# A hybrid decoder block: where the attention groups are combined, and how early four kinds of loads are asked for

## The chip, the cores and the metric

The kernel runs on one core of a Trainium2 chip. The metric is the time of one execution on the device in microseconds; the kernel before takes 2662.7 us (median of three runs, 2660.01 to 2666.11). A core has a matrix engine (TensorE, PE in the profile, its weight loads PEld), a vector engine (DVE), an activation engine (ACT), a general engine (POOL) and a queue engine (SP). Each works through its own queue in order; they wait for each other through semaphores. DMA transfers are issued from the queues of SP, ACT and POOL.

## What is computed

The reference is one layer on 2048 tokens of width 1024, in float32. From `h = rmsnorm(x)` one projection gives q, k, v for 12 heads, u and z for a gated unit, and two gates:

```
q, k = rope(...), rope(...);  u = gelu(...);  z = gelu(...)
gate_a, gate_b = sigmoid(...), sigmoid(...)
for g, (window, dilation) in enumerate(((128,1), (512,4), (2048,16))):
    o[g], lse[g] = dilated_window_attention(q[g], k[g], v[g])
y_attn = sum_g softmax_g(lse)[g] * o[g]                     # "combine"
y_gmlp = u * (tril(w_spatial) @ layernorm(z) + b_spatial)   # per chunk of 128 tokens
merged = gate_a * (y_attn @ w_branch_attn) + gate_b * (y_gmlp @ w_branch_gmlp)
x = x + rmsnorm(merged @ w_out)
x = x + rmsnorm(relu(rmsnorm(x) @ w_mlp_in)**2 @ w_mlp_out)
```

## The kernel before

Every large product is made in three matmuls of 128x512 from operands split in a high and a low part (`split`, line 68: the high part by one engine at L70 or L72, the low part at L78; `mm3`, L95 to L97). The tokens are worked on in four chunks of 512, numbered 0 to 3, two halves of two chunks. PE's order is written out by hand: each helper yields after three matmuls, and a call `steps(n)` takes n such steps from a generator (`filler`) that holds the projections for u, z and the gates. The order of the other engines is made by a planner from the order in the program, its own clock and what each instruction waits for; `behind()` makes what it holds come after the last instruction traced so far on each of these engines.

The stages in the order of time:

1. q, k and v of all tokens (up to about 470 us), then u and z of the second half.
2. `gates()` (L703): u and gate projections that are left, 126 pieces `t` of 12 matmuls, some with sums of operands that save products (phases `PHASES`). A piece's weights are loaded by `piece` (L627, four pieces ahead) and split by `split_piece` (three ahead) into places of two tiles `spots`, `t % 8`, or `t % 4` in the last phase, which starts at `LAST` = 116. A finished bank is copied by ACT (L722, `i == 1`) or added by DVE (L727 to L741) and stored (L717). One more load from the list `ins` goes out per piece (L720). From step 12 of it on, the attention's 48 units run between these steps, each a chain PE, DVE, ACT, PE.
3. When attention is done (about 958 us), 75 steps of the gates are left. `combined` there interleaves them with `combine(c)` of chunks 2 and 3: five parts, which load `A` (L961), form the factors (L964 to L977), scale (ACT L982, DVE L985), add (L987, L988), and transpose on PE (L993) and store `ya` (ACT L996, L997).
4. z of the first half: two chunks of 32 steps of PE, with its weights `w_z0` and the operand `hT_b` reloaded from DRAM through `ins`, and eight more pieces `zin` for the second chunk. Chunks 0 and 1 are combined beside it through one tile `cw`, at the steps that `todo` names. The branch weights `wb` are loaded and split here too.
5. For each chunk in the order 2, 3, 0, 1: `merge` (eight blocks `dt`, two products with a gate each, drained by DVE at L1174) and `out_block` (`w_out`, the norm, the transposes). The operands `yt` of a merge are loaded and split by `load_y`, the first time by POOL alone. A gate is loaded by `load_gate` (L1148) into a pool of three and two places and passed through the sigmoid by ACT (L1157). Beside the first merge `sz_out` makes the spatial product of chunks 0 and 1 (L551, L558, L561), which loads u as `ur` (three places), and `w_out` is split.
6. The feed-forward part (from about 1370 us), which the change does not touch.

Of the kernel before, what the change touches and what calls it, by code (L numbers as in the profile page):

```python
# [41 lines left out]
def block_kernel(ctx, tc, a, out):  # L42
# [503 lines left out]
    def sz_out(zp, zt, c):  # L546
        wsp, bsp, lngb = sgu[c // 2]
        for g in range(4):
            p = psum_aux(f"sz_{c}{g}")
            for i in range(4):  # L550
                pe.matmul(p[:, i * P:(i + 1) * P], zt[:, i, g * P:(g + 1) * P], wsp[:, g, :],  # L551
                          start=True, stop=True)
            t = zp.tile([P, 512], F32, name=f"sb_{c}{g}", tag="sz", bufs=2 if c > 1 else 5)
            ut = zp.tile([P, 512], F32, name=f"ur_{c}{g}", tag="ur", bufs=2 if c > 1 else 3)
            sp.dma_start(ut, u_d[g, :, c * 512:(c + 1) * 512])
            bb = bsp[:, g, :]
            bb = bass.AP(tensor=bb.tensor, offset=bb.offset, ap=[list(bb.ap[0]), [0, 4], [1, P]])
            dve.scalar_tensor_tensor(t.rearrange("p (c i) -> p c i", i=P),  # L558
                                     p.rearrange("p (c i) -> p c i", i=P), lngb[:, 0, g:g + 1], bb,
                                     op0=OP.mult, op1=OP.add)  # L560
            (dve if c == 3 or c < 2 and g % 2 else pool).tensor_mul(t, t, ut)  # L561
            sp.dma_start(yg_d[g, :, c * 512:(c + 1) * 512], t)
# [24 lines left out]
    def want(q):  # L587
        if q < len(queue) and q not in loaded:
            wi, kind, n, half = queue[q]
            if kind == "z":  # L590
                if half and not n:
                    loaded[q] = load_wide(wi, "w_z1")
                    for kk in range(2):
                        sp.dma_start(wz_d[kk], f32(loaded[q][kk]))
                elif not n:
                    loaded[q] = wide_tiles("w_z0")
                    return [(f32(loaded[q][kk])[:, o], wz_d[kk][:, o]) for kk in range(2) for o in range(2)]
            else:
                loaded[q] = load_w(wi, f"w_{kind}{n}{half}")

# [29 lines left out]
    def split_piece(t):  # L630

        if t >= len(seq):
            return
        if t == 4:
            g_["spots"].append(wp.tile([P, 4, 2, 4, P], F32R, name="spots1", tag="w", bufs=3))
        at_ = t % 4 if t >= LAST else t % 8
        w = g_["spots"][at_ // 4][:, at_ % 4]
        split(w[:, 0], w[:, 1], g_["raw"].pop(t).rearrange("p (k c) -> p k c", k=4),
              "act" if t < 12 else "pool", "pool")
        g_["w"][t] = w  # L640
# [21 lines left out]
    def gates():  # L662
# [12 lines left out]
        for t, (half, i, n) in enumerate(seq):  # L675
            if t in starts:
                ph, t0 = starts[t], t
                if ph + 1 < len(phases):
                    s = (ph + 1) % 2
                    if not slots[s]:  # L680
                        slots[s] = hp.tile([P, 2, 2, 4, 512], F32R, name="opA", tag="hT", bufs=2)
                    for j, i2 in enumerate(phases[ph + 1][1]):
                        new = operand(phases[ph + 1][0], i2, slots[s][:, j])
                        ins += new[0]
                        todo += new[1]
                else:
                    ws, hs = want(5), reload_h(0)
                    ins += ws[:2] + hs[:4] + ws[2:] + hs[4:]
            elif todo and (t - t0) % 3 == 1 and t > t0 + 1:
                w, k = todo.pop(0)  # L690
                with behind():
                    split(w[:, 0, k:k + 2], w[:, 1, k:k + 2], f32(w)[:, 1, k:k + 2], "act", "pool")
            if t == LAST:
                g_["ends"] = g_["vs"] + zs[8:]
            for n_ in (t + PIECES,) if t < LAST else {0: (4, 5), 1: (6, 7), 2: (8,), 3: (9,)}.get(t - LAST, ()):
# [19 lines left out]
            x, z, fn = xs[n], zs[n], AF.Copy if n < 8 else AF.Gelu_apprx_tanh  # L715
            while out_:
                sp.dma_start(*out_.pop())  # L717
            for _ in range(2 if half and i == 4 or t in (LAST + 5, LAST + 6) else 1):
                if ins:
                    sp.dma_start(*ins.pop(0))  # L720
            if i == 1:
                act.activation(x, p, AF.Copy)  # L722
            elif i == 2:
                act.activation(z, p, fn)
                o = z, 0, 0
            elif i == 6:
                dve.tensor_add(z, x, p)  # L727
            elif i == 7:
                dve.tensor_add(x, x, p)
            elif i == 5:  # L730
                if (half, n) == (0, 0):
                    g_["vs"] = a[9:11]
                v = g_["vs"].pop(0)
                g_["vs"].append(v)
# [26 lines left out]
    def filler():  # L761

        for q, (wi, kind, n, half) in enumerate(queue):
            if kind == "z" and n == 1:
                continue
            if kind == "g":
                yield from gates()
                want(q + 1)
                cw.append(wp.tile([P, 4096], F32, name="cw", tag="w", bufs=3))
                next(cs[2])  # L770
                continue
            if q not in loaded:
# [182 lines left out]

    def combine(c):

        A = cb.tile([P, 4, 3, 264], F32, name=f"A_{c}", tag="cA", bufs=2) if c > 1 else \
            cw[0][:, :3168].rearrange("p (n g e) -> p n g e", n=4, g=3)
        for g in range(3):  # L960
            sp.dma_start(A[:, :, g, :], att_d[g][c * 512:(c + 1) * 512, :].rearrange("(n p) e -> p n e", p=P))  # L961
# [28 lines left out]
        for m in range(2):  # L990
            pt = psum_aux(f"yt_{c}{m}")
            for i in range(4):
                pe.transpose(pt[:, i * P:(i + 1) * P], A[:, i, 0, m * P:(m + 1) * P], ident)  # L993
            yt = cb.tile([P, 512], F32, name=f"ya_{c}{m}", tag="cya", bufs=2) if c > 1 else \
                st.tile([P, 512], F32, name=f"ya_{c}{m}", tag="ev", bufs=3)
            act.activation(yt, pt, AF.Copy)  # L996
            act.dma_start(ya_d[m, :, c * 512:(c + 1) * 512], yt)  # L997
# [56 lines left out]
            with behind():  # L1054
                next(cs[k])

    combined((0, 0), (4, 1), (14, 0), (4, 0), (4, 0), (10, 0), (2, 1), (4, 1), (4, 1), (10, 1))
    steps(75 - 56)
    ec.close()
    ega.close()  # L1060

# [16 lines left out]
    next(sg)  # L1078
    while not cw:
        steps(1)  # L1080
    todo = {14: (2,), 16: (2,), 18: (2,), 28: (2, 3), 40: (3,), 42: (3,), 45: (3,), 54: (3,)}
    for n in range(1, 56):
        steps(1)
        if zin:
# [58 lines left out]
                load_wo(n // 2)  # L1143

    def load_gate(c, dt, wch):
        if (c, dt, wch) not in gates:
            gt = gtp.tile([P, 512], F32, name=f"g{wch}_{c}{dt}", tag=f"gt{wch}", bufs=3 - wch)
            sp.dma_start(gt, gate_d[wch * 8 + dt, :, c * 512:(c + 1) * 512])  # L1148
            gates[c, dt, wch] = gt

    opened = set()

    def open_gate(c, dt, wch):
        if (c, dt, wch) not in opened:
# [5 lines left out]
    def merge(c, yt, between, each=None):  # L1160
        cs = slice(c * 512, (c + 1) * 512)
        mg = []
        for dt in range(KT):
# [11 lines left out]
                parts.append(gt)  # L1175
            dve.tensor_add(parts[0], parts[0], parts[1])
            split(mg[-1][:, 0, dt % 4, :], mg[-1][:, 1, dt % 4, :], parts[0])
            if dt < KT - 1:
                for wch in range(2):
                    open_gate(c, dt + 1, wch)  # L1180
# [278 lines left out]
    def spatial_out(dt):  # L1459
# [4 lines left out]
        if dt == 1:  # L1464
            ez.close()
            mgp.append(stack(e2, "mg1", 1))
            ttp = stack(e2r, "ttp", 2, side="right")
            load_wo(2)
            load_wo(3)
# [17 lines left out]
    for n, c in enumerate(chunks):  # L1487
        if n:
            mg = merge(c, yt, {0: flush, 2: flush}, merge_sums if c == 0 else merge_sums_last if c == 1 else None)
        for i in range(4):  # L1490
# [4 lines left out]
                sums_ahead(1 + i // 2)  # L1495
            if n < 3 and not i:
                yt = load_y(chunks[n + 1])
                for dt in range(2):
                    for wch in range(2):
                        load_gate(chunks[n + 1], dt, wch)  # L1500
            if n == 3 and i == 1:
                e2r.close()
                rx = stack(e3, "rx", 1, side="right")
                spare = rx.tile([P, 512], F32, name="ar1_4", tag="xs", bufs=LEAD + 1)
                r3 = stack(er, "r3", 1, side="right")
# [557 lines left out]
```

## Time and profile before

| | |
|---|---|
| median of three runs | 2662.7 us |
| profiled execution, its own time | 2661.19 us |
| its span, first to last instruction | 2659.4 us |
| mean granted clock of TensorE | 0.995 |
| PE busy | 2617.5 us (98%) |
| DVE, ACT, POOL busy | 1649.7, 1087.4, 1201.2 us |
| DMA, mean over the span | 199 GB/s |

The profile is of one execution. A row of a timeline gives the start, the duration, the engine, the line, the operation, what it writes and reads, its shape, a count, and in brackets the idle time before it and what ended it. A row of the waits gives the waiting engine and line, what it waited for, the total in us, how often and the longest. A row of windows gives a stretch, its length and then the busy time of PE, PEld, DVE, ACT and POOL with their instructions, the granted clock (1.00 is full), the DMA engines' busy share and the rate in GB/s.

### The profile page before, as it was taken

To read this page: it belongs to the slowest core of one execution; us is meant where nothing else is said; L and a number is where in the kernel's file an instruction comes from. 1 tells how busy PE (TensorE), PEld (TensorE's weight loads), DVE (VectorE), ACT (ScalarE), POOL (GpSimd) and SP (SyncE) were. 2 spreads that over 40 slices of the span, in tenths; PEclk is the share of its full clock that TensorE was granted. 3 is DMA by queue.
4 is the path that set the end of the run, shared out by engine and by line. 5 is a ranking of instruction groups with operands and counts; after the bars stand their busy time and mean duration, and the time that the engine had idled before them with its cause. 6 is when DMAs were issued, how large, how long until landed. Compare 5 with 4: busy or idle time off the path is not lost. (4 is left out here: it accounts for less than half of the span.)

```text
span 2659.4 us, 35499 instructions
## 1 busy us (share of the span) xinstructions
PE 2617.5 (98%) x12458; PEld 2185.1 (82%) x12458; DVE 1649.7 (62%) x2793; ACT 1087.4 (41%) x2279; POOL 1201.2 (45%) x1089
## 2 busy tenths in 40 slices
PE   9999999999999998899999999999999999999998
PEld 8888888888888886788778788888888888888887
DVE  5676665534443455755576655645437888888866
ACT  5213111254455433444445555655545333323334
POOL 0363354374454563311324463233215776676645
PEclk9999999999999999999999999999999999999999
DMA  8779768888888998744566464643343222222235
GB/s 321 283 245 325 265 228 291 294 280 251 291 287 236 240 297 328 248 137 153 205 212 252 138 225 152 220 145 119 118 148 107 87 68 75 88 88 87 88 111 214
DMA packets 389284, 528.29 MB, mean 199 GB/s; under 512 B 57009, under 2 KB 242097, under 8 KB 387570
## 3 DMA queue, kind: packets, MB, share of 16 engines
q1 hardware_dynamic: 300336, 436.03, 49.8%
q0 software_dynamic: 14992, 51.65, 5.1%
q10 hardware_dynamic: 73778, 38.35, 4.7%
q8 instruction: 98, 1.61, 0.2%
q14 instruction: 80, 0.66, 0.1%
HBM read 342.77 MB, written 183.17 MB: 198 GB/s over the span
## 5 line engine op out<-in xcount | busy, mean ns | idle before, releaser
L1914 PE MATMUL ya<-T_spots,s 128*128 128x512 f32 x1176 | 289.3, 389 | 0.7 <-ACT T_spots L70 0.5
L70 ACT ACTIVATE s<-sraw 128x768 fp32r<-128x768 f32 (+1 forms) x184 | 127.2, 696 | 330.3 <-POOL sraw L1715 155.6
L1914 PEld LDWEIGHTS ya<-T_spots,s 128*128 128x128 f32 x1176 | 220.6, 188 | 47.3 <-ACT T_spots L70 0.9
L78 DVE TENSOR_TENSOR s<-sraw,s 128x512 fp32r<-128x512 f32 x172 | 184.1, 1095 | 8.5 <-ACT s L70 4.6
L1387 PE MATMUL aa<-B,A 128*128 128x512 f32 x768 | 182.2, 390 | 0.8 <-DVE A L85 0.7
L1358 POOL TENSOR_TENSOR s<-w1r 128x512 f32<-128x512 f32 x32 | 42.3, 1322 | 309.7 <-DVE S L78 263.2
L703 PE MATMUL g<-opA,spots 128*128 128x512 f32 x672 | 170.0, 397 | 0.0
L1387 PEld LDWEIGHTS aa<-B,A 128*128 128x128 f32 x768 | 143.9, 188 | 31.3 <-DVE A L85 1.1
L703 PE MATMUL g<-opB,spots 128*128 128x512 f32 x648 | 164.0, 397 | 0.0
L1914 PE MATMUL yc<-T_spots,s 128*128 128x512 f32 x624 | 159.7, 389 | 0.0
L95 PE MATMUL x<-hT_a,wq 128*128 128x512 f32 x384 | 149.7, 390 | 0.0
L96 PE MATMUL x<-hT_a,wq 128*128 128x512 f32 x384 | 149.4, 389 | 0.0
L97 PE MATMUL x<-hT_a,wq 128*128 128x512 f32 x384 | 149.4, 389 | 0.0
L703 PEld LDWEIGHTS g<-opA,spots 128*128 128x128 f32 x672 | 121.2, 188 | 21.8
L78 POOL TENSOR_TENSOR spots<-gr,spots 128x512 fp32r<-128x512 f32 x98 | 127.6, 1306 | 22.9 <-DMA gr<-in_w_in_dram 15.9
L1914 PEld LDWEIGHTS yc<-T_spots,s 128*128 128x128 f32 x624 | 117.1, 188 | 24.3
L703 PEld LDWEIGHTS g<-opB,spots 128*128 128x128 f32 x648 | 116.9, 188 | 21.1
L70 ACT ACTIVATE hl<-r 128x512 fp32r<-128x512 f32 x48 | 30.4, 633 | 235.3 <-POOL r L321 89.0
L72 POOL TENSOR_SCALAR spots<-gr 128x512 fp32r<-128x512 f32 x86 | 54.8, 637 | 140.1 <-PE g L703 99.6
L952 DVE TENSOR_REDUCE o<-po 128x256 f32<-128x512 f32 x48 | 33.2, 692 | 133.5 <-PE po L951 133.5
L1714 POOL TENSOR_TENSOR sraw<-sraw 128x256 f32<-128x256 f32 x56 | 41.8, 747 | 161.8 <-DVE s L78 158.8
L78 POOL TENSOR_TENSOR T_spots<-w2r,T_spots 128x512 fp32r<-128x512 f32 x70 | 104.4, 1520 | 7.3 <-ACT T_spots L70 7.3
(424 smaller groups left out, 6962.5 us busy)
## 6 DMA issues: line engine op xcount, KB each, us to landing
w1r<-in_w_mlp_in_dram SPq DMA_DIRECT2D x64, 512.0 KB, 3.8
sraw<-sd SPq DMA_DIRECT2D x128, 256.0 KB, 3.3
qk<-hl SPq DMA_DIRECT2D x24, 1024.0 KB, 5.7
qq<-qk SPq DMA_DIRECT2D x96, 256.0 KB, 5.0
w2r<-in_w_mlp_out_dram SPq DMA_DIRECT2D x16, 1024.0 KB, 7.8
sd<-u ACTq DMA_DIRECT2D x63, 256.0 KB, 3.6
g<-gated SPq DMA_DIRECT2D x58, 256.0 KB, 3.9
gr<-sgd SPq DMA_DIRECT2D x53, 256.0 KB, 4.8
```

The lines of the kernel that those rows point to most:

```text
L70: act.activation(hi, src, AF.Copy)
L72: pool.tensor_scalar(hi, src, 1.0, 1.0, op0=OP.mult, op1=OP.mult)
L78: (pool if lo_eng == "pool" else dve).tensor_sub(lo, src, f32(hi))
L95: pe.matmul(ps, lh, rh, start=start, stop=False)
L96: pe.matmul(ps, lh, rl, start=False, stop=False)
L97: pe.matmul(ps, ll, rh, start=False, stop=stop)
L703: pe.matmul(p, w[:, l, k], h[:, r, k], start=i in (1, 6, 5, 4) and not k and not m, stop=k == 3 and m == 2, skip_group_check=True)
L952: dve.tensor_reduce(ot[:, :, j * 64:(j + 1) * 64], po.rearrange("p (b h e) -> p b e h", b=4, h=2), axis=AX.X, op=OP.add)
L1358: pool.tensor_add(s1, a21, a22)
L1387: pe.matmul(p, w[:, l, k, :], h[:, r, k, :], start=i in (1, 6, 5) and not k and not n, stop=k == 3 and n == 2, skip_group_check=True)
L1714: pool.tensor_add(a22, a21, a22)
L1914: pe.matmul(p, s[:, l], w[r], start=i in (1, 2, 5) and not m and not o, stop=m == 1 and o == 2, skip_group_check=True)
```

## The change

The parts: `combined` beside the gates now takes chunks 2, 3 and 0 in 62 of the 75 steps (before: 2 and 3 in 56), with a third buffer `A`, and only chunk 1 goes through `cw` beside z. The first four of z's weight loads, each cut in two, are put on the list four pieces before `LAST`, which frees the second tile of `spots` eight pieces earlier (four places instead of eight from then on). In the first phase of the gates' second half of the tokens, six of the copies out of a bank go from ACT to DVE. `ur` has four places instead of three for the chunks 0 and 1. From the second merge on, gates have eight places instead of five: eight loads are issued at the first output block before the merge, and each block loads the gates of three and five blocks further on.

```
-            ut = zp.tile([P, 512], F32, name=f"ur_{c}{g}", tag="ur", bufs=2 if c > 1 else 3)
+            ut = zp.tile([P, 512], F32, name=f"ur_{c}{g}", tag="ur", bufs=2 if c > 1 else 4)
...
-                    return [(f32(loaded[q][kk])[:, o], wz_d[kk][:, o]) for kk in range(2) for o in range(2)]
+                    return [(f32(loaded[q][kk])[:, o, k:k + 2], wz_d[kk][:, o, k:k + 2])
+                            for kk in range(2) for k in (0, 2) for o in range(2)]
...
-        at_ = t % 4 if t >= LAST else t % 8
+        at_ = t % 4 if t >= LAST - 8 else t % 8
...
-                    ws, hs = want(5), reload_h(0)
-                    ins += ws[:2] + hs[:4] + ws[2:] + hs[4:]
+                    hs = reload_h(0)
+                    ins += hs[:4] + ws[4:6] + hs[4:6] + ws[6:] + hs[6:]
...
+            if t == LAST - 4:
+                ws = want(5)
+                ins += ws[:4]
...
-            for _ in range(2 if half and i == 4 or t in (LAST + 5, LAST + 6) else 1):
+            for _ in range(2 if half and i == 4 or t in (LAST + 5, LAST + 7) else 1):
...
-            if i == 1:
+            if i == 1 and half and n > 1:
+                dve.tensor_copy(x, p)
+            elif i == 1:
                 act.activation(x, p, AF.Copy)
...
-                next(cs[2])
+                next(cs[3])
...
-        A = cb.tile([P, 4, 3, 264], F32, name=f"A_{c}", tag="cA", bufs=2) if c > 1 else \
+        A = cb.tile([P, 4, 3, 264], F32, name=f"A_{c}", tag="cA", bufs=3) if c != 1 else \
             cw[0][:, :3168].rearrange("p (n g e) -> p n g e", n=4, g=3)
...
-    combined((0, 0), (4, 1), (14, 0), (4, 0), (4, 0), (10, 0), (2, 1), (4, 1), (4, 1), (10, 1))
-    steps(75 - 56)
+    combined((0, 0), (4, 1), (10, 0), (3, 0), (3, 0), (2, 2), (8, 0), (0, 1), (3, 1), (3, 1), (10, 1),
+             (0, 2), (3, 2), (3, 2), (10, 2))
+    steps(75 - 62)
...
-    todo = {14: (2,), 16: (2,), 18: (2,), 28: (2, 3), 40: (3,), 42: (3,), 45: (3,), 54: (3,)}
+    todo = {14: (3,), 16: (3,), 18: (3,), 28: (3,)}
...
     def load_gate(c, dt, wch):
-        if (c, dt, wch) not in gates:
-            gt = gtp.tile([P, 512], F32, name=f"g{wch}_{c}{dt}", tag=f"gt{wch}", bufs=3 - wch)
+        if dt < KT and (c, dt, wch) not in gates:
+            d = chunks.index(c) * KT + dt
+            pl, tag = (gtp, f"gt{wch}") if c == 2 or d % (5 - 2 * wch) < 3 - wch else (gxp[0], f"gx{wch}")
+            gt = pl.tile([P, 512], F32, name=f"g{wch}_{c}{dt}", tag=tag, bufs=3 - wch if pl is gtp else 2 - wch)
...
             split(mg[-1][:, 0, dt % 4, :], mg[-1][:, 1, dt % 4, :], parts[0])
+            if c != 2:
+                load_gate(c, dt + 5, 0)
+                load_gate(c, dt + 3, 1)
...
-                for dt in range(2):
-                    for wch in range(2):
-                        load_gate(chunks[n + 1], dt, wch)
+                for dt, wch in ((0, 0), (0, 1), (1, 0), (1, 1), (2, 0), (2, 1), (3, 0), (4, 0)):
+                    load_gate(chunks[n + 1], dt, wch)
```

More of the change, by code (lines that the diff above doesn't have):

```diff
@@ L993, in combine @@
                 pe.transpose(pt[:, i * P:(i + 1) * P], A[:, i, 0, m * P:(m + 1) * P], ident)
-            yt = cb.tile([P, 512], F32, name=f"ya_{c}{m}", tag="cya", bufs=2) if c > 1 else \
+            yt = cb.tile([P, 512], F32, name=f"ya_{c}{m}", tag="cya", bufs=2) if c != 1 else \
                 st.tile([P, 512], F32, name=f"ya_{c}{m}", tag="ev", bufs=3)
@@ L1145, in load_gate @@
     def load_gate(c, dt, wch):
-        if (c, dt, wch) not in gates:
-            gt = gtp.tile([P, 512], F32, name=f"g{wch}_{c}{dt}", tag=f"gt{wch}", bufs=3 - wch)
+        if dt < KT and (c, dt, wch) not in gates:
+            d = chunks.index(c) * KT + dt
+            pl, tag = (gtp, f"gt{wch}") if c == 2 or d % (5 - 2 * wch) < 3 - wch else (gxp[0], f"gx{wch}")
+            gt = pl.tile([P, 512], F32, name=f"g{wch}_{c}{dt}", tag=tag, bufs=3 - wch if pl is gtp else 2 - wch)
             sp.dma_start(gt, gate_d[wch * 8 + dt, :, c * 512:(c + 1) * 512])
             gates[c, dt, wch] = gt
-    opened = set()
+    opened, gxp, egx = set(), [], ExitStack()
     def open_gate(c, dt, wch):
@@ L1466, in spatial_out @@
             mgp.append(stack(e2, "mg1", 1))
+            gxp.append(stack(egx, "gx", 1))
             ttp = stack(e2r, "ttp", 2, side="right")
@@ L1497, in block_kernel @@
                 yt = load_y(chunks[n + 1])
-                for dt in range(2):
-                    for wch in range(2):
-                        load_gate(chunks[n + 1], dt, wch)
+                for dt, wch in ((0, 0), (0, 1), (1, 0), (1, 1), (2, 0), (2, 1), (3, 0), (4, 0)):
+                    load_gate(chunks[n + 1], dt, wch)
             if n == 3 and i == 1:
                 e2r.close()
+                egx.close()
                 rx = stack(e3, "rx", 1, side="right")
```

## The prediction

> **What bounds it now.** I read the page's busy times first, then the matrix engine's waits, then windows over the stages, then single rows where a stage lost time.
>
> ```profile
> PE 2617.5 (98%) x12458; PEld 2185.1 (82%) x12458; DVE 1649.7 (62%) x2793; ACT 1087.4 (41%) x2279; POOL 1201.2 (45%) x1089
> ...
> PE yt L993 <- issue: 11.5, 1, 11.5
> PE b L95 <- DVE g L1174: 5.3, 4, 2.2
> ...
> PE g L703 <- ACT ga L722: 1.6, 1, 1.6
> ...
> PE g L703 <- ACT gx L722: 0.6, 1, 0.6
> ```
>
> TensorE (PE) is the bound: 2659.4 - 2617.5 leaves 42 us of idle time, and the change adds and removes no matmul. So it can win only idle time and time at a lowered clock. One wait, L993, holds 11.5 us of it. The next view gives stretches: length, busy time of PE, weight loads, DVE, ACT, POOL, then the granted clock, the DMA share and GB/s.
>
> ```profile
> 950.00:962.00 12.00, 12.00 (x64) 10.07 (x64) 3.45 (x5) 1.20 (x2) 7.26 (x8) 1.00 0.77 250
> 962.00:1010.40 48.40, 48.40 (x223) 40.16 (x222) 27.93 (x53) 17.45 (x46) 25.68 (x20) 1.00 0.98 336
> 1010.40:1019.00 8.60, 6.13 (x22) 3.87 (x21) 0.69 (x1) 0.63 (x1) 0.00 (x0) 0.86 1.04 405
> 1019.00:1058.00 39.00, 37.06 (x155) 29.56 (x154) 25.37 (x63) 16.98 (x37) 9.71 (x12) 0.94 0.94 334
> 1058.00:1070.00 12.00, 2.36 (x10) 2.30 (x11) 9.43 (x6) 3.56 (x14) 11.92 (x8) 0.63 0.08 29
> ...
> 1070.00:1080.00 10.00, 10.00 (x43) 8.18 (x42) 2.87 (x11) 5.61 (x7) 3.57 (x4) 0.94 0.52 171
> ```
>
> The last gates run to 1010.4 with PE full; the z stage of the first half of the tokens follows, to 1076.4. It is 192 matmuls at the pitch of a full PE, (23.43 - 0.39) / 101 = 0.228 us from the first row below, so 43.8 us, and some 2.5 us of transposes and row sums; it takes 66.0. Some 20 us are lost there.
>
> ```profile
> 958.13 23.43 PE L703 MATMUL g<-opA,spots 128*128 128x512 f32 x102
> 982.75 1.03 PE L993 MATMUL yt<-ident,A 128*128 128x128 f32 x8
> ...
> 1018.67 0.80 PE L97 MATMUL z<-w_z,hT_b 128*128 128x512 f32 x1 [0.67 <-DMA hT_b<-hbd]
> ...
> 1067.64 1.94 PE L993 MATMUL yt<-ident,cw 128*128 128x128 f32 x8 [11.53 <-issue]
> ...
> 1076.44 0.39 PE L95 MATMUL b<-yt,wb 128*128 128x512 f32 x1
> ```
>
> **Part 1, the second chunk beside z leaves.** Now two chunks are combined beside z through one buffer, cw, the second at steps 28 to 54 of 55. Its loads go out at 1044.99, DVE starts at 1052.62 and ends its sum at 1067.53; the transposes that PE meets in order wait for that.
>
> ```profile
> 1044.99 2.20 SPq L961 DMA_DIRECT2D cw<-att  x3
> ...
> 1052.62 0.17 DVE L964 TENSOR_TENSOR M<-cw 128x16 f32<-128x16 f32 x1
> ...
> 1066.09 1.44 DVE L988 TENSOR_TENSOR cw<-cw 128x1024 f32<-128x1024 f32 x1
> ```
>
> After the change only one chunk is left there, at steps 14 to 28, where the first one stands today without a wait. So 11.53 us of idle go, and the slow clock behind them: from the restart at 1067.64 to 1070 at about half rate (1.2 us lost) and 0.06 x 10 = 0.6 in the next stretch. **-13.3 us** (bounds -13.3 and -11.5, if the clock is lost to something else).
>
> **Part 2, three chunks beside the gates, and z's weights sooner.** Now two are combined there, with 14 to 20 steps (of three matmuls, 0.684 us) per chunk; after it three, each 16 steps behind the one before. The rows of the two chains:
>
> ```profile
> 969.39 0.18 DVE L965 TENSOR_TENSOR M<-M,A 128x16 f32<-128x16 f32 x1 [0.63 <-DMA A<-att]
> ...
> 976.75 1.54 DVE L988 TENSOR_TENSOR A<-A 128x1024 f32<-128x1024 f32 x1
> ...
> 995.94 1.21 DVE L988 TENSOR_TENSOR A<-A 128x1024 f32<-128x1024 f32 x1
> ...
> 983.39 1.09 ACT L996 ACTIVATE ya<-yt 128x512 f32<-128x512 f32 x2 [0.45 <-PE yt L993]
> ...
> 986.22 0.24 ACT L969 ACTIVATE E<-E 128x48 f32<-128x48 f32 x1
> ```
>
> First chain: data at 969.39, done at 978.29; its transposes move from step 36 to step 30, 958.13 + 30 x 0.684 = 978.65. The slack is 0.4 us, and the loads of A come later, since 2 MB of z's weights (the first four of now eight pieces, with four more issues of about 0.4 us on SP) go ahead of them: at 336 to 405 GB/s 5 to 6 us, of which the idle DMA time in 950:962, 0.23 x 12 = 2.8 us, takes half. About 2 us late: a wait of 1.6. Later chains: the exponential is queued on ACT behind the copies of the chunk before, so a chain begins at the previous transposes; now 982.75 to 997.15, 14.4 us, against 16 x 0.684 + 0.8 = 11.7 given. A wait of up to 2.7 each, or none, as today's chain was spread over 20 steps; I take 1 each. While DVE waits for A, the gates' sums queue behind it; four banks, 8.2 us of PE, cover them. What else moves with the third chunk: three issues of A on SP (some 0.5 us each, ahead of the gates' stores, for which nobody waits), two of ya on ACT's queue, 16 small products on ACT and about 7 us of sums on DVE; these two are busy for 17.45 and 27.93 of the 48.4 us, so the engines have room and only the chain's length counts.
>
> Against this stands the start of z. Today the product at 1018.67 (the 21st of z, due at 1010.43 + 20 x 0.228 = 1015.0) waits for the last piece of hT_b, 3.7 us, and the clock of 0.94 over 39 us costs 2.3 more: 6.0 in all. The queue was full (0.98, 1.04), so the last piece lands when all bytes ahead have moved. Chunk 0's 1.6 MB join them (4.0 to 4.8 us); the 2 MB that start sooner find 2.8 us idle before 962 and some 2 later. The last piece lands about when it does now. PE's waits beside the gates (3.6 in sum) then only take what it would have waited at z. Sum for both: **-1 us**; bounds -6 (chains fit, pieces land in time) and +5 (three waits of 2.7 with their clock, the 4.4 us not hidden).
>
> Of the lowered clock the trace says that a short wait suffices:
>
> ```profile
> 1107.30 0.50 PE L95 MATMUL b<-yt,wb 128*128 128x512 f32 x1 [1.77 <-DVE g L1174]
> ...
> 1110.00:1120.00 10.00, 10.00 (x40) 7.90 (x38) 6.37 (x9) 5.36 (x8) 1.58 (x3) 0.89 0.83 300
> ```
>
> A wait of 1.77 us is followed by 0.11 x 10 = 1.1 us of lost clock (and some before 1110). The Trainium skill's "TensorE: Matmul & The Clock Gate" (Part 1) has the rate fall to half after at least one idle window of about 3.4 us, and warns of gaps above 3; by that the waits here, each below 3 us, would cost no clock, and this sum would be about -3 instead of -1. The row contradicts it, and I go by the row.
>
> **Part 3, what is late next.** With PE 14 us earlier at the merge, POOL's splitting of its operands yt is not.
>
> ```profile
> 1051.58 0.90 SPq L91 DMA_DIRECT2D yt<-yad  x2
> ...
> 1056.70 0.62 POOL L72 TENSOR_SCALAR yt<-yt 128x512 fp32r<-128x512 f32 x1
> 1057.41 2.20 POOL L78 TENSOR_TENSOR yt<-yt 128x512 fp32r<-128x512 f32 x1
> ...
> 1071.02 2.55 POOL L78 TENSOR_TENSOR yt<-yt 128x512 fp32r<-128x512 f32 x2
> ...
> 960.34 1.28 POOL L78 TENSOR_TENSOR spots<-gr,spots 128x512 fp32r<-128x512 f32 x1
> ```
>
> Six pairs take 1056.70 to 1073.57, 16.9 us, beside DVE's large sums; alone a pair is 0.62 + 1.28 = 1.9, six 11.4. The loads come about 1 us sooner without cw's bytes ahead (they wait for weights that z paces). POOL ends between 1067 and 1072.6; I take 1068.5, nearest to alone, as DVE's sums are gone. PE begins the merge at 1076.44 - 14.3 = 1062.1 and needs the last pair after 15 of 18 matmuls, at 1065.6. A wait of 2.9: **+3 us** (bounds +1.4 and, with clock, +8.7).
>
> **Part 4, the fourth place for u** in the spatial product:
>
> ```profile
> 1104.72 1.33 DVE L561 TENSOR_TENSOR sb<-sb,ur 128x512 f32<-128x512 f32 x1 [1.01 <-DMA ur<-ud]
> ```
>
> That late load holds DVE just before the product that PE awaits at 1107.30; 1.77 + 1.7 of clock. One more load stands ready; a later wait for w_out's weights may remain. **-3 us** (0 to -3.5).
>
> **Part 5, eight places for the merges' gates.** ACT waits for gate loads today, PE through DVE behind it:
>
> ```profile
> ACT g L1157 <- DMA g<-gated: 54.6, 38, 4.8
> ...
> SPq L1192 <- DMA x1d<-xr: 111.8, 11, 15.8
> ```
>
> Eight are issued at the first output block, four or more blocks ahead of their use, no byte more. PE's other three waits for L1174 go: 5.3 - 1.8 = **-3.5 us** (0, if SP holds the new loads behind its wait for xr, to -3.8).
>
> **Part 6, six copies from ACT to DVE** in the first phase of the gates:
>
> ```profile
> 541.16 0.75 DVE L558 SCALAR_TENSOR_TENSOR sb<-sz,lngb,bsp 128x512 f32<-128x512 f32 x1 [8.93 <-DMA ygd<-sb]
> ...
> 552.43 0.96 PE L703 MATMUL g<-hT_a,spots 128*128 128x512 f32 x3 [1.63 <-ACT ga L722]
> ```
>
> The two L722 waits go, **-1.8 us** (-2.2 at best). Queued behind 541.16, the copy that PE awaits at about 537 would come 5 us late: +6. Four places instead of eight for pieces of the gates, eight products earlier: a split of 1.9 us has three products, 8.2 us; nothing, or 1.9 for each that comes late.
>
> **Sum:** -13.3 - 1 + 3 - 3 - 3.5 - 1.8 = -19.6. The profiled execution took 2661.19 us (span 2659.4): 2641.6. It stands 1.5 below the median 2662.7, so **2643**.
>
> **Rivals.** (a) POOL keeps today's pace at yt: +8.7 for +3, and part 2 at +1: 2651. For: DVE still splits two weights there. Against: its large sums are gone. (b) The copies stall behind DVE's spatial product: +6 for -1.8, 2651. For: DVE is in order and idle 8.93 there. Against: that product's wait is known to the planner too. (c) z starts in time and the chains fit: -6 for -1, 2637. For: the 2 MB sooner. Against: the full queue. A smaller form, in which PE's short waits beside the gates keep the full clock, is part 2 at -3, 2641; its chance is inside the forecast's, and the row after 1107.30 speaks against it. It is what the Trainium skill's page "TensorE: Matmul & The Clock Gate" would give. (d) Slower: a chain beside the gates does not fit 16 steps and opens a gap like today's, 11.53 + 1.8 us. One leaves a gain of 6; from two on (+26.6, 2670) it ends slower. For: the same operations in the same order, POOL and DMA busier. Against: it ran there twice without one. (e) Mixed small losses leave nothing.
>
> **Chances.** Forecast 0.50, (a) 0.15, (b) 0.12, (c) 0.10, (d) 0.08, (e) 0.05. A run can tell about 0.2%, 5.3 us, from no change: faster 0.87, same 0.05, slower 0.08. The likeliest case's own range is 2636 to 2649; with (a), (b) and part of (c) 2634 to 2656.
>
> **What would show it.** Right: no idle time of several us at L993 after 1040; a wait of about 3 us at the first products of the merge, put down to POOL; hardly any waits of ACT for gate loads; the last gates' transposes waiting for L988 by 1 to 3 us, and z's first products for hT_b by less than now. Wrong: a clock under 0.9 over 960:1010, a wait at the first gates above 2 us, or gate loads still late.

## The result and the profile after

The changed kernel takes 2669.33 us (median of 17 runs, 2665.86 to 2673.16) where the kernel before takes 2661.06 beside it (17 runs, 2655.65 to 2666.11): 1.0032 of before, 95% interval 1.0024 to 1.0039. It is 0.3% slower; the forecast was 2643 us, 0.7% faster. The profiled execution after the change has a span of 2665.1 us, 5.7 more than the one before.

The busy times of the page and the waits of PE after the change (total, times, longest):

```profile
PE 2622.6 (98%) x12458; PEld 2190.0 (82%) x12458; DVE 1657.0 (62%) x2799; ACT 1085.6 (41%) x2273; POOL 1192.4 (45%) x1089
...
PE yt L999 <- issue: 9.3, 3, 3.2
PE b L95 <- DVE g L1183: 5.7, 2, 5.0
PE g L707 <- DVE ga L726: 4.3, 1, 4.3
PE b L96 <- POOL yt L78: 3.7, 4, 1.3
...
PE z L97 <- DMA hT_b<-hbd: 1.8, 1, 1.8
```

The one wait of 11.5 us at the transposes is gone, and three of 3 us stand in its place; a wait of 4.3 for the new copies on DVE, one of 5.0 in the merge and four for POOL's yt have joined them. The lines have moved: L993 is now L999, L703 L707, L722 L726 and L1174 L1183.

The stages show where that lies. First before, then after: the last 75 steps of the gates, z, the merge of the first chunk up to its first output product, and the four output blocks behind it. The columns are as in the windows of the prediction.

```profile
958.10:1010.40 52.30, 52.30 (x241) 43.38 (x240) 29.31 (x55) 17.45 (x46) 27.58 (x22) 1.00 0.96 332
1010.40:1076.40 66.00, 51.96 (x211) 40.93 (x210) 36.36 (x71) 23.46 (x53) 25.20 (x22) 0.87 0.75 271
1076.40:1120.40 44.00, 41.95 (x209) 35.08 (x208) 35.53 (x56) 21.41 (x31) 10.31 (x10) 0.96 0.84 280
1120.40:1167.20 46.80, 46.00 (x209) 37.67 (x210) 27.67 (x61) 22.42 (x47) 4.66 (x7) 1.00 0.47 159
```

```profile
963.80:1030.00 66.20, 56.94 (x250) 46.37 (x249) 42.10 (x73) 25.17 (x67) 32.77 (x30) 0.95 0.89 299
1030.00:1077.70 47.70, 45.88 (x204) 37.12 (x203) 25.73 (x53) 15.53 (x32) 10.86 (x13) 1.00 0.88 303
1077.70:1133.00 55.30, 46.54 (x209) 37.46 (x208) 44.92 (x60) 26.42 (x39) 18.59 (x20) 0.88 0.79 266
1133.00:1178.30 45.30, 45.30 (x209) 37.68 (x209) 23.92 (x57) 20.09 (x43) 4.67 (x7) 1.00 0.40 139
```

z became 18.3 us shorter, at full clock. The gates before it became 13.9 longer, the first merge 11.3. With the first gates (442.2 to 446.6, +4.4), the rest of the merges (244.0 to 240.8, -3.2), the output blocks (-1.5) and the two stretches that the change does not touch (+1.3 and -2.2) that is the difference of the spans.

**The gates.** The transposes of the three chunks beside the gates, then rows of DVE, ACT and POOL from the first and the second chain, then the two scalings of each chunk in the kernel after and before (shortest, median, longest in ns):

```profile
987.46 1.07 PE L999 MATMUL yt<-ident,A 128*128 128x128 f32 x8 [2.96 <-issue]
1004.16 1.06 PE L999 MATMUL yt<-ident,A 128*128 128x128 f32 x8 [3.14 <-issue]
1020.90 1.06 PE L999 MATMUL yt<-ident,A 128*128 128x128 f32 x8 [3.17 <-issue]
```

```profile
974.45 1.08 DVE L970 TENSOR_TENSOR M<-A 128x16 f32<-128x16 f32 x1 [2.82 <-DMA A<-att]
...
992.90 0.69 DVE L744 TENSOR_TENSOR ga<-ga,g 128x512 f32<-128x512 f32 x1 [4.95 <-PE g L707]
993.51 1.47 DVE L978 TENSOR_TENSOR Z<-E,A 128x16 f32<-128x16 f32 x3
...
996.21 3.87 DVE L991 TENSOR_TENSOR A<-A,E 128x1024 f32<-128x1024 f32 x2
...
1002.84 1.21 DVE L994 TENSOR_TENSOR A<-A 128x1024 f32<-128x1024 f32 x1
```

```profile
988.12 1.09 ACT L1002 ACTIVATE ya<-yt 128x512 f32<-128x512 f32 x2 [1.92 <-DMA ud<-cv]
...
990.91 0.24 ACT L975 ACTIVATE E<-E 128x48 f32<-128x48 f32 x1
```

```profile
996.16 1.29 POOL L78 TENSOR_TENSOR spots<-ga,spots 128x512 fp32r<-128x512 f32 x1
```

```profile
L991 DVE TENSOR_TENSOR A<-A,E x6: 1212/1964/2319, 979.8 to 1015.2; 128x1024 f32<-128x1024 f32 x6
```

```profile
L985 DVE TENSOR_TENSOR A<-A,E x4: 1218/1224/1632, 972.0 to 991.5; 128x1024 f32<-128x1024 f32 x4
```

The second chain's last sum (1002.84) ends at 1004.05, and its transposes start at 1004.16: PE waits for the end of DVE's chain. The first chain starts late, as DVE waits 2.82 us for A. From one transposition to the next there are 16.7 us, and 16 steps give 11.7. Three things make the later chains long. The exponential (990.91) begins behind the copies of the chunk before (988.12). The sum Z (993.51) stands on DVE behind the drain of a gate block whose matmuls PE makes only after its wait (4.95 us idle), 2.4 us after the exponential's end, so that a wait of PE delays the next chain. And the pair of scalings takes 3.87 us; the second chain before the change, also beside a split of POOL, took 2.77 for its pair. There the split began 0.12 us after the first scaling, here 0.05 us before it, and that scaling takes 2.32 us instead of 1.23. The Trainium skill's "SBUF — State Buffer" (Who interferes with whom) says that a DVE instruction with two inputs from SBUF and a GpSimd instruction that reads SBUF block each other; these rows fit that.

**The copies.** The second of DVE's new copies stands behind the spatial product, which waits for ygd:

```profile
543.58 0.75 DVE L558 SCALAR_TENSOR_TENSOR sb<-sz,lngb,bsp 128x512 f32<-128x512 f32 x1 [9.05 <-DMA ygd<-sb]
...
548.22 0.68 DVE L726 COPY ga<-g 128x512 f32<-128x512 f32 x1
```

```profile
549.04 1.19 PE L707 MATMUL g<-hT_a,spots 128*128 128x512 f32 x2 [4.27 <-DVE ga L726]
```

**The first merge.** POOL waits for u, and the issue of w_out's raw weights on its queue stands behind that; DVE's part of the split comes late, and with it the drain that PE needs:

```profile
1103.90 1.29 POOL L561 TENSOR_TENSOR sb<-sb,ur 128x512 f32<-128x512 f32 x1 [5.39 <-DMA ur<-ud]
1105.15 0.60 POOL L1122 DMA_DIRECT2D woraw<-in_w_out_dram  x1
```

```profile
1124.41 1.23 DVE L78 TENSOR_TENSOR wo<-woraw,wo 128x1024 fp32r<-128x1024 f32 x1 [2.26 <-ACT wo L70]
1125.55 1.88 DVE L1183 TENSOR_TENSOR g<-g,b 128x512 f32<-128x512 f32 x3
```

```profile
1126.29 0.79 PE L95 MATMUL b<-yt,wb 128*128 128x512 f32 x1 [5.03 <-DVE g L1183]
```

### The profile page after: what moved, and what is told of

It is laid out like the page before. It is cut to its first block, busy times and chain, and to the rows that moved or that the text cites. A ratio compares the mean times of both kernels' runs of the same rounds, so it can differ in the third digit from the quotient of the medians.

```text
span 2665.1 us, 35494 instructions
## 1 busy us (share of the span) xinstructions
PE 2622.6 (98%) x12458; PEld 2190.0 (82%) x12458; DVE 1657.0 (62%) x2799; ACT 1085.6 (41%) x2273; POOL 1192.4 (45%) x1089
## 5 line engine op out<-in xcount | busy, mean ns | idle before, releaser
L707 PE MATMUL g<-opA,spots 128*128 128x512 f32 x672 | 171.9, 400 | 0.0
L707 PE MATMUL g<-opB,spots 128*128 128x512 f32 x648 | 165.6, 400 | 0.0
L707 PEld LDWEIGHTS g<-opA,spots 128*128 128x128 f32 x672 | 122.2, 190 | 22.1
L707 PEld LDWEIGHTS g<-opB,spots 128*128 128x128 f32 x648 | 118.0, 190 | 21.5
```

The lines of the kernel that those rows point to most:

```text
L707: pe.matmul(p, w[:, l, k], h[:, r, k], start=i in (1, 6, 5, 4) and not k and not m, stop=k == 3 and m == 2, skip_group_check=True)
```

## The experiments

All ratios are to the kernel before, run beside each kernel, with the 95% interval; 0.1% is 2.7 us. A ratio is not the quotient of the two medians, from which it differs by up to 0.0005. The stages are those of each kernel's one profiled execution, between the same matmuls: A from the first gates to the end of attention, B the last 75 steps of the gates, C z, D the first chunk's merge and output blocks, E the other merges and output blocks.

| kernel | ratio | A | B | C | D | E |
|---|---|---|---|---|---|---|
| before | 1 | 442.3 | 52.3 | 66.0 | 90.7 | 244.0 |
| changed | 1.0032 (1.0024 to 1.0039) | 446.6 | 66.2 | 47.7 | 100.7 | 240.8 |
| u_copies | 1.0022 (1.0014 to 1.0031) | 442.4 | 68.1 | 46.3 | 99.7 | 242.6 |
| u_space | 1.0016 (1.0004 to 1.0028) | 446.4 | 56.1 | 51.7 | 100.3 | 241.5 |
| u_yt | 1.0041 (1.0027 to 1.0054) | 447.2 | 68.2 | 49.0 | 97.3 | 240.5 |
| u_ur | 1.0025 (1.0016 to 1.0034) | 447.0 | 67.1 | 46.2 | 94.0 | 240.7 |
| b_copies | 1.0023 (1.0013 to 1.0033) | 445.9 | 52.3 | 64.6 | 90.6 | 243.7 |
| b_ur | 1.0016 (1.0004 to 1.0028) | 441.2 | 52.3 | 67.7 | 91.8 | 241.0 |
| b_gates | 1.0008 (0.9997 to 1.0018) | 442.6 | 52.3 | 62.9 | 91.6 | 240.7 |
| b_gates2 | 1.0003 (0.9994 to 1.0012) | 441.3 | 52.3 | 66.4 | 93.1 | 239.9 |
| b_three | 1.0005 (0.9993 to 1.0017) | 442.0 | 66.5 | 46.3 | 94.9 | 242.9 |
| best1 | 0.9976 (0.9967 to 0.9985) | 442.6 | 54.9 | 53.6 | 96.0 | 241.2 |
| best1_g5 | 0.9978 (0.9968 to 0.9987) | 443.1 | 56.1 | 51.2 | 93.6 | 242.6 |
| best1_ws | 0.9987 (0.9978 to 0.9996) | 441.9 | 56.3 | 54.1 | 95.8 | 240.9 |

One execution is not the median: the profiled one of before (2661.19 us) lies 2 to 3 us above the medians of before in these comparisons (2657.9 to 2659.4), and those of u_ur and b_gates are 6 us below their own medians.

### Six copies, undone and alone

```
-            if i == 1 and half and n > 1:
-                dve.tensor_copy(x, p)
-            elif i == 1:
+            if i == 1:
                 act.activation(x, p, AF.Copy)
```

> The changed kernel with its six copies back on ACT, the rest as changed. Theory (the rival (b) of the prediction): the second copy stood on DVE behind the spatial product that waits for ygd, and that costs PE 4.3 us of waiting and about 1.5 of clock in the first phase of the gates; here the wait for DVE's copy (4.3 in one, from L726) is gone and two short waits for ACT (1.6 and 0.6) are back: the time falls by 3 to 5 us. The other view: the 4.3 us only takes the place of a wait that comes a little later for the same data; then the time moves by less than 1.5 us.

2664.44 us. Stage A is back at 442.4, and the waits are those of before:

```profile
PE g L707 <- ACT ga L726: 1.6, 1, 1.6
```

4.2 us of the profile went as the first theory said; the ratio to before fell by 0.0010, 2.7 us, with an uncertainty of 3. The same edit alone in the kernel before settles it.

> The kernel before with only the six copies moved from ACT to DVE (part 6). The prediction's term: -1.8 us (bounds -2.2 and +6). The theory from the trace of the changed kernel: PE waits 4.3 us for the second copy, behind DVE's product that waits for ygd, and a lowered clock follows; against the 1.8 us saved that is +2.5 to +5 us. The rival: nothing measurable, within 1 us.

2663.29 us, 0.23% over before (0.13 to 0.33), which is 6 us. Stage A is 3.6 longer, by the same wait:

```profile
PE g L703 <- DVE ga L722: 4.0, 1, 4.0
```

Part 6 costs 3.6 to 4.4 us in the stage where it acts; the ratio says 3.5 to 9.

### The spacing of the chains

```
-    combined((0, 0), (4, 1), (10, 0), (3, 0), (3, 0), (2, 2), (8, 0), (0, 1), (3, 1), (3, 1), (10, 1),
-             (0, 2), (3, 2), (3, 2), (10, 2))
-    steps(75 - 62)
+    combined((0, 0), (4, 1), (12, 0), (4, 0), (4, 0), (2, 2), (8, 0), (2, 1), (4, 1), (4, 1), (10, 1),
+             (2, 2), (4, 2), (4, 2), (10, 2))
+    steps(75 - 74)
```

> The changed kernel with the three chains beside the gates 20 steps apart instead of 16 (they fill 74 of the 75 steps instead of 62). Theory A: a chain needs about 14.4 to 16.6 us and 16 steps give 11.7, 20 give 14.5; the waits at the transposes (9.3 us in three) fall below 3, no lowered clock follows them, and as the pieces of hT_b are issued behind the drains of the gates, they come sooner too: the time falls by 7 to 12 us. Theory B (the prediction's part 2): the last piece of hT_b lands at the same time whatever PE does, so the wait moves to the start of z: waits at the transposes below 3, but 4 to 7 us at the first products of z, and the time falls by less than 4. Theory C: the chains are slow because DVE and POOL slow each other and A comes late, not because of their spacing: the waits stay above 6 us and the time moves by less than 3.

2662.08 us, 0.16% (4.3 us, uncertain by 3.8) less than as changed. The waits at the transposes are 1.4 us in all, and z waits twice:

```profile
PE z L97 <- DMA hT_b<-hbd: 2.7, 1, 2.7
...
PE yt L999 <- issue: 1.4, 1, 1.4
...
PE z L95 <- DMA hT_b<-hbd: 1.1, 1, 1.1
```

B fell by 10.1 and C grew by 4.0. Theory C falls; the truth lies between A and B: the chains were too close, and some 4 of the 10 us come back at the start of z. The last piece of hT_b is not bound to one time on the clock. PE's product that waits for it came at 1018.67 before, at 1036.46 as changed and at 1027.91 here, each time 6.5 to 8.9 us after z's first product (1010.43, 1029.99, 1019.01). The last issue stands on SP's queue between the stores of the last gates; it went out at 1009.65 before, at 1018.51 here, and as changed at

```profile
1030.83 0.43 SPq L724 DMA_DIRECT2D hT_b<-hbd  x1
```

### yt's high parts on ACT

```
-    yt = load_y(2, ("pool", "pool"))
+    yt = load_y(2, ("act", "pool"))
```

> The changed kernel with the high parts of the first merge's operands yt made by ACT instead of POOL. Theory: POOL's twelve operations (12.4 us) are what the merge of the first chunk waits for (3.7 us of waiting and about 1.4 of clock at its start); with six of them on ACT they end 3 to 4 us sooner, the wait for POOL falls below 1 us and the time by 3 to 5 us. The other view: PE then waits for the next thing, a weight split or the drain that DVE makes at that place; the wait for POOL goes and the time falls by less than 1.5 us.

2670.23 us, no gain. ACT reaches its six high parts only behind the last activation of z (1080.10), and PE's first product of the merge waits for them:

```profile
1082.21 3.21 ACT L70 ACTIVATE yt<-yt 128x512 fp32r<-128x512 f32 x6
```

```profile
1082.97 0.47 PE L95 MATMUL b<-yt,wb 128*128 128x512 f32 x1 [2.91 <-ACT yt L70]
```

The wait for POOL fell from 3.7 to 1.8 us and one of 2.9 for ACT took its place: the second view.

### The fourth place for u, undone and alone

```
-            ... tag="ur", bufs=2 if c > 1 else 4)
+            ... tag="ur", bufs=2 if c > 1 else 3)
```

> The changed kernel with three places for the spatial factor u instead of four. Theory: with four places, four loads of u are issued together in the merge of the first chunk, behind the stores of the products before them; POOL waits for one of them, and its issues of w_out's raw weights stand behind that, 4 to 10 us later in the merge than before; that gives the second wait of this merge (5.2 us at the products of b). With three places it falls back to 2 to 3 us, the time by 2 to 4 us. The other view: the whole chain of the merge is later in its stage because PE reaches the stage 14 us sooner than the loads; then the wait stays above 4 us and the time is the same within 1.5 us, or up to 2 us longer.

2665.33 us. In the profile stage D fell by 6.7, and the wait for DVE's drain in the merge, 5.7 us as changed, is small; another stands at the first output product:

```profile
PE o L95 <- ACT g L1166: 3.5, 1, 3.5
...
PE b L95 <- DVE g L1183: 0.9, 2, 0.5
```

The ratio fell by only 0.0007 (1.9 us, uncertain by 3.1), and the profiled execution is the fastest of the twelve. That the four kernels with four places and the chunk moved have D at 97.3 to 100.7, and the five with three places and the chunk moved at 93.6 to 96.0, speaks for the theory; its size stays between 2 and 7 us. POOL's wait of 5.39 is gone, and the issue of w_out's raw weights that stood behind it (1105.15, 27.5 us into the merge) goes out 19.3 us into it. Part of the gain lies where the theory did not look, at the start of the merge: the wait for POOL's yt is 1.8 us here and 3.7 as changed. The loads of u go out ahead of the last three of w_branch and of yt. With four places the first load of yt was issued 8.0 us before the merge's first product (1069.70), with three 10.8. In the four other kernels with three places and the chunk moved it is 10.1 to 11.1, in u_copies and u_space 8.7 and 7.9 (in u_yt 11.2, of which 2.9 are PE's wait for ACT). Why the three issues of w_branch between them took 9.5 us as changed and 6.5 here is not shown.

> The kernel before with only the fourth place for u (part 4). The prediction's term: -3 us (0 to -3.5): a load stands ready and the wait of 1.8 us with its clock in the first merge goes. The theory after seeing the changed kernel: the fourth load is issued only together with the others, behind the stores of the products, so POOL and the issues of w_out's raw weights behind it are later: 0 to +4 us.

2662.32 us, 1.0016 (1.0004 to 1.0028): no gain of 3, and a loss if anything. In its profile the first merge and its output blocks are 1.1 us longer than before. The larger differences lie where the edit changes nothing: 4.4 us more ahead of the first gates (520.3 against 515.9), 3.0 less in E. So part 4 is worth nothing at best; that it costs 4 us alone is not shown.

### Eight places for the gates alone

The hunks of `load_gate`, `gxp` and the eight loads at the first output block, put into the kernel before; the second time is the same kernel again.

```
+            pl, tag = (gtp, f"gt{wch}") if c == 2 or d % (5 - 2 * wch) < 3 - wch else (gxp[0], f"gx{wch}")
...
+            if c != 2:
+                load_gate(c, dt + 5, 0)
+                load_gate(c, dt + 3, 1)
...
+                for dt, wch in ((0, 0), (0, 1), (1, 0), (1, 1), (2, 0), (2, 1), (3, 0), (4, 0)):
...
```

> The kernel before with only the eight places for the merges' gates (part 5). The prediction's term: -3.5 us, since three waits of PE for DVE's drains in the later merges go (bounds 0 to -3.8). The rival: in the kernel as changed these waits went for another reason or come back elsewhere; then the time is within 1 us of before.

> The kernel before with only the eight places for the merges' gates once more. The first time its profile showed the stage lengths 5 us shorter (the waits in the last two merges gone) while its median was 1.4 us over before's. If the profile is typical, the median comes to 2 to 5 us under before's now; if the median was, this profile shows what the place of those waits took.

2660.80 and 2657.73 us: 1.0008 and 1.0003. E is 3.3 and 4.1 us shorter, by the size that the term said. D is 0.9 and 2.4 longer. Before and b_gates2, in the same part of the first merge: SP's queue, ACT's part of a w_out split, and the first output product.

```profile
1108.48 11.57 SPq L1148 DMA_DIRECT2D g<-gated  x6
...
1116.78 1.06 ACT L70 ACTIVATE wo<-woraw 128x1024 fp32r<-128x1024 f32 x1 [1.05 <-DMA woraw<-in_w_out_dram]
...
1120.45 0.47 PE L95 MATMUL o<-wo,mg 128*128 128x512 f32 x1 [0.33 <-DVE g L1174]
```

```profile
1107.86 13.21 SPq L1150 DMA_DIRECT2D g<-gated  x9
...
1117.81 1.06 ACT L70 ACTIVATE wo<-woraw 128x1024 fp32r<-128x1024 f32 x1 [2.03 <-DMA woraw<-in_w_out_dram]
...
1121.47 0.76 PE L95 MATMUL o<-wo,mg 128*128 128x512 f32 x1 [3.59 <-ACT g L1159]
```

The places are free from the first merge on, so the planner puts three of the next merge's loads there, ahead of w_out's raw weights; these come 1.0 us later, and the first output product too. There PE waits 3.6 us instead of 0.3, and is slowed after it. (The row names ACT's sigmoid; the drain of DVE behind the split is what came last before it.) The first merge is bound by w_out's chain at that point, and the wait of 1.8 us that part 4 was to remove lay ahead of the same bound. The intervals of the two ratios allow a gain of 0.8 and 1.6 us at most, and the table says why. E is 239.9 to 242.6 us in the nine kernels with eight places (mean 241.0) and 241.0 to 244.0 in the five with five (mean 242.8), and before has the longest of all: eight places win about 1.9 us there and not 3.5. They give 0.9 and 2.4 back in D here, and 2.4 in best1 against best1_g5 below, so that nothing is left.

### The chunk moved, alone

The hunks of `combined`, `todo`, the third buffer `A` and z's weights, without the copies, u's fourth place and the gates' places.

> The kernel before with only the move of the chunk from z to the gates and z's weights sooner (parts 1 and 2 and what follows, part 3); copies, u's places and the gates' places as before. The prediction's terms: -13.3 - 1 + 3 = -11.3 us. The theory from the trace of the changed kernel: z 18 us shorter, the last gates 14 longer, the first merge 4 to 6 longer by its wait for yt: within -3 and +4 us of before. Should it gain 7 us or more, the move is sound and the loss comes from the other parts.

2659.43 us: 1.0005 (0.9993 to 1.0017), as the theory from the changed kernel's trace had it, not 11.3 us faster. B is 14.2 longer, C 19.7 shorter, D 4.2 longer, and the three waits are there without the other parts, as is the one for POOL's yt:

```profile
PE yt L997 <- issue: 9.5, 3, 3.2
...
PE b L96 <- POOL yt L78: 2.4, 4, 1.3
```

### All three repaired

best1 is the changed kernel with the edits of u_copies, u_space and u_ur together.

> The changed kernel with the copies back on ACT, the chains 20 steps apart and three places for u, all three together. If their gains add (by the runs before this one 2.6, 4.3 and 1.9 us of the ratio to before), it comes to 0.1% under the time of before, give or take 0.1%: 2652 to 2660 us where before has 2658. If two of them only moved the same wait, it stays 0.1 to 0.2% above before.

2654.45 us: 0.24% under before (0.15 to 0.33), 0.56% (14.9 us, uncertain by 3) under the changed kernel. The three gains alone add to 8.9 us, each uncertain by 3 to 4, so together they gave somewhat more than was expected. So the loss came from these three places, and the move itself is sound. Two runs undo one more part of it each.

> The changed kernel with copies on ACT, chains 20 steps apart and three places for u, and in addition five places for the merges' gates as before, so part 5 undone in the version that is faster than before. The prediction's term says it is 3.5 us slower than the same with eight places (0.9976 of before), that is 0.9989, with waits of PE for DVE's drains in the last three merges back (2 to 2.5 us each with the clock). The rival: those waits are only sometimes there, and the time is the same within 1.5 us.

Five places for the gates: 2651.37 us, 0.9978. Eight places give nothing here either: E is 1.4 longer without them, D 2.4 shorter. Against b_three this kernel differs only in the spacing, and it is 0.27% (7.2 us, uncertain by 4) faster: the price of 16 steps instead of 20.

```
-                    return [(f32(loaded[q][kk])[:, o, k:k + 2], wz_d[kk][:, o, k:k + 2])
-                            for kk in range(2) for k in (0, 2) for o in range(2)]
+                    return [(f32(loaded[q][kk])[:, o], wz_d[kk][:, o]) for kk in range(2) for o in range(2)]
...
+                    ws, hs = want(5), reload_h(0)
+                    ins += ws[:2] + hs[:4] + ws[2:] + hs[4:]
...
```

> The changed kernel with copies on ACT, chains 20 steps apart and three places for u, and z's weights loaded as before (four pieces of 1 MB, the first after the last phase of the gates begins), so half of part 2 undone. Theory A, the queue is full there and only the bytes ahead count: the last piece of hT_b lands at about the same time, the wait at the start of z stays (3.9 and 1.4 us) and the time is the same within 2 us. Theory B, the earlier start uses idle time of the queue: without it the last piece lands 3 to 5 us later and the time grows by 3 to 5 us.

z's weights as before: 2653.18 us, 0.9987 (0.9978 to 0.9996). That is 0.11% more than best1, uncertain by 0.13; B and C together are 1.9 us longer. The ratio puts the worth of the earlier start between nothing and 6 us, the profile at 2; the runs don't separate theory A from B.

## Why the prediction was wrong

**Part 1 (-13.3): right.** The wait of 11.5 and the slow clock behind it are gone. Of the 18.3 us that z lost, 1.0 are the eight transposes that moved away and about 4 are z's start (6.0 before; after, a wait of 1.8 and a clock of 1.00); 13 remain.

**Part 2 (-1): the step that failed.** It read the chain right (14.4 us against 11.7, "a wait of up to 2.7 each, or none"), and then took 1 us for each of the later two and 1.6 for the first. The waits were 2.96, 3.14 and 3.17 at PE, and the stretch lost 0.05 x 66.2 = 3.3 us of clock besides: 12.6 us, against some 4 won at z's start, so about +8.5, over the upper bound of +5. The low end, chains that fit as today's with 20 steps did, was no case for 16 steps; the row of today's chain was the nearest and said 2.7. What came on top is the drain queued ahead of Z (2.4 us) and the slower scalings (3.87 us a pair against 2.77). The second step that failed is that the last piece of hT_b lands when it does now, because the queue is full: the product that waits for it came at 1036.46 and not at 1018.67, and with 20 steps at 1027.91. Its issue stands between the stores of the last gates, so it moves with PE. Rival (d) was this mechanism with the wrong size: not one gap like 11.53, but three of 3 us. That its 2670 lies beside the measured 2669 is luck, as parts 3, 4 and 6 made up the rest.

**Part 3 (+3): the wait came, near its size, partly by luck.** In b_three, without parts 4 to 6, PE waits 2.4 us for POOL's yt and D is 4.2 longer. POOL's twelve operations took 12.4 us as changed, nearest to alone, as chosen. But the loads of yt did not come 1 us sooner; they went out 18 us later, at 1069.70 for 1051.58:

```profile
1069.70 0.90 SPq L91 DMA_DIRECT2D yt<-yad  x2
```

They stand on SP's queue behind the loads of w_branch, whose first went out at 1042.05 for 1024.65, after the later end of the gates. So POOL began only at 1074.78, 2.9 us ahead of the merge. PE came late too, at 1077.67 where 1062.1 was forecast, and the two errors nearly cancel. With four places for u the wait is 3.7, and a stretch at about half rate follows (the first row below, at most 0.48 x 7 = 3.4 us, as 1.3 of the wait lie in it).

```profile
1084.00:1091.00 7.00, 5.70 (x20) 4.46 (x20) 6.01 (x8) 1.20 (x2) 3.15 (x4) 0.52 0.82 287
1125.00:1132.00 7.00, 5.71 (x14) 4.51 (x15) 6.55 (x10) 5.65 (x9) 0.53 (x1) 0.52 0.72 234
```

**Part 4 (-3): wrong.** The wait behind the late u lay in front of w_out's chain, which bounds the same merge; alone it won nothing, and with the chunk moved it cost 2 to 7 us, in part by holding POOL's queue, on which w_out's raw weights are issued. In the changed kernel the wait there is 5.0 us and the second row above adds up to 3.4 of clock, where the prediction had 3.5 in all for the kernel before; and yt comes later with it. D is 5.8 longer than in b_three, what part 5 adds there included.

**Part 5 (-3.5): the number came in E, the mechanism did not.** E fell by 3.2 and PE's waits for the drains there from 3.5 to 0.7 us. But the gate loads were to come early, with hardly any waits of ACT for them, and that sign failed. Before they were 54.6 us in 38 waits; after:

```profile
ACT g L1166 <- DMA g<-gated: 49.7, 34, 4.6
```

In the second merge SP still issues ten gate loads one after another over 20.2 us, before over 20.6; why the free places don't let them go sooner is not tested. And 3.2 is a lucky pair of profiles: over all kernels E differs by 1.9. "No byte more" was true and not enough: some of the same bytes go earlier, into the one merge that is bound by loads. Three comparisons of medians show no gain.

**Part 6 (-1.8): rival (b) came true.** The row of 541.16 with its 8.93 us of idle was quoted; the planner did not keep the copy ahead of the product. +4.4 in place of -1.8, near the upper bound of +6.

By these sizes the sum is -13.3 + 8.5 + 4.2 + 5.8 - 3.2 + 4.4 = +6.4, of which the two untouched stretches take 0.9 back (the profile says 5.7, the ratio 8.5). Against the -19.6 of the prediction part 2 has 9.5 of the 26 us, part 4 some 9, part 6 6 and part 3 1. (Rival (c), -6 for -1, gives 2638 and not 2637; nothing hangs on it.) best1, in which parts 2, 4 and 6 are repaired, is about 6 us faster than before and not 20. In its profile B and C together are 9.8 us shorter, where parts 1 and 2 said 14.3, as z still waits 3.8 and 0.9 us for hT_b; D is 5.3 longer, where parts 3 and 4 said 0, as the first merge still waits for yt (1.6) and its first output product for the chain of w_out (3.7, as in b_gates2); and part 6 wins nothing.

**The lowered clock.** The prediction let a wait of under 3 us cost clock, by one row. Behind the three waits at the transposes (2.96, 3.14 and 3.17 us) the changed kernel's windows have

```profile
988.00:992.00 4.00, 4.00 (x14) 3.23 (x13) 0.00 (x0) 3.45 (x5) 2.96 (x4) 0.57 0.86 283
1005.00:1009.00 4.00, 4.00 (x14) 3.17 (x12) 1.25 (x6) 2.44 (x4) 0.19 (x1) 0.57 0.94 300
1021.00:1025.00 4.00, 4.00 (x22) 3.44 (x23) 0.64 (x2) 2.37 (x3) 0.00 (x0) 1.00 0.91 338
```

Two cost 1.7 us of clock each (0.43 x 4), and the longest cost none. The traces of the fourteen kernels have the clock at half, between 30 and 2600 us, for 3.41 us or for two, three or four times that. In the five kernels with chains 16 steps apart and waits of 2.96 to 3.20 us at the transposes, 11 of these 14 waits were followed by such a stretch and 3 by none. So neither the row nor the rule of the Trainium skill's "TensorE: Matmul & The Clock Gate" that was quoted there gives the cost of a single wait of this length.

## What to carry to other kernels

Where a chain is put beside other work, measure its length in the nearest row and give it that many steps, and treat a shortfall as a wait at every repetition, with the clock behind it; four steps more per chunk were worth 7 us here. Before a wait is counted as won, look for the next bound of the same stage (here w_out's loads), and before a load is moved ahead, look what is queued behind it there. An operation moved to another engine in order waits for all that stands in that queue: one row with 9 us of idle time at the place is enough to leave it where it is.

## What the runs showed of the hardware

A two-input operation of DVE on 128x1024 took 2.32 us where a split of POOL had begun 0.05 us before it (996.16 above). Where DVE's had begun first, POOL's split took 2.14 us (at 999.10) instead of 1.29. In u_space, where POOL had ended its last split 1.3 us earlier, the third chunk's two took 1.18 each.

A wait of PE can lengthen the next wait of PE: the drain that DVE must make ahead of the next chain's sum hangs on matmuls behind the first wait. Executions of unchanged code differ by a few us: up to the first gates' matmuls, which no edit touches, the profiles range from 515.8 to 520.8 us, so a gain of 3 us is read from the stage where it arises and not from one execution's total.
